# Wide moving operands in the first FFN's partial sums and in the mixer's projections

## The chip, the cores and the metric

The kernel runs on one core of a Trainium2 chip. The metric is device time in microseconds (us) of one execution; the shown time is the median of three runs. The engines are TensorE (PE: matmuls; its weight loads are PEld in the profile), VectorE (DVE), ScalarE (ACT), GpSimd (POOL) and SyncE (SP, which here only issues DMAs).

## The reference

One residual block on 256 tokens of width 2048, batch 1, all in float32. `mod` is a LayerNorm followed by a scale and a shift that are computed from a conditioning vector `c`.

```python
mod = (jax.nn.silu(c) @ w_ada[l] + b_ada[l]).reshape(B, N_SUBLAYERS, 3, D_MODEL)
y = _swiglu(modulate(x, 0), ffn1_w13[l], ffn1_w2[l])        # D_FF = 5632
x = _layer_norm(ALPHA * x + FFN_WEIGHT * gate[:, 0, None, :] * y, ln_g[l, 0], ln_b[l, 0])
u = modulate(x, 1)
proj = u @ w_in[l] + b_in[l]       # q, k, v, o, gates, x_rg, g_rg
h_m = _mlstm(...)                  # 4 heads of 256
h_r = _rg_lru(_causal_depthwise_conv(x_rg, ...), ...) * jax.nn.gelu(g_rg)
y = jnp.concatenate([h_m, h_r], axis=-1) @ w_out[l]
x = _layer_norm(ALPHA * x + gate[:, 1, None, :] * y, ln_g[l, 1], ln_b[l, 1])
y = _swiglu(modulate(x, 2), ffn2_w13[l], ffn2_w2[l])
x = _layer_norm(ALPHA * x + FFN_WEIGHT * gate[:, 2, None, :] * y, ln_g[l, 2], ln_b[l, 2])
```

with `_swiglu(u, w13, w2) = (silu(u @ w13_g) * (u @ w13_v)) @ w2`.

## The kernel before, in words

**Two-part products.** Every weight tile (128 x 2048 floats, 1 MB) is loaded by SP into one of four raw buffers, cast by ACT into a high part (line 95) and completed by DVE with a low part, the difference (line 97); there are three buffers of each part. The activations u are kept in two parts as well, `uh` and `ul` (lines 158 and 159), with the contraction on partitions: 16 blocks (KT) of 128 rows by 256 tokens. A product is three matmuls: high x high, high x low, low x high.

**Two forms of matmul.** In `stat_w` (lines 259 to 268) a block of 128 x 128 weights is stationary and the 256 tokens move: 128x256 out, features on partitions. In `mov_t` (lines 270 to 280) 128 tokens are stationary and 512 columns of weights move: 128x512 out, tokens on partitions. The profile tells them apart by line (266 to 268, 277 to 279).

**The conditioning.** Rows of w_ada are 144 tiles of 1 MB ("ada"), each multiplied with silu(c) and summed along the row by one DVE instruction (line 173). They go through the same SP queue and the same four raw buffers as the weights. `tick` (line 181) is called at each weight load and slips in ada tiles at a set rate per load: `RAMP_RATE` for each stage of the ramp, `FFN1_RATE` in the rest of the first FFN, `MIX_RATE` and `FFN2_RATE` later. `ada_until` issues at once all that a following step needs. Scale and shift of one block of u need two ada tiles.

**The ramp** (lines 571 to 647). The first FFN can't have all of u at its start, since u needs 32 ada tiles. So the first 24 of its 44 row blocks (each 128 columns of gate and of value) are worked off in five stages over the contraction: `STAGES` = 2, 2, 4, 4, 4 of the 16 blocks of u. A stage goes through 12 quads (2 row blocks, gate and value, in two PSUM banks) with `stat_w`. At the end of a quad its two sums are copied by ACT (first stage, line 642) or added by DVE (line 644) into a buffer in SBUF: the space of yacc, gate and x serves for that. Quads 6 and 7 instead keep four of the eight PSUM banks over the whole ramp. Shortly before a stage ends, `modulate` (lines 232 to 247) makes the next stage's blocks of u: transposes on PE, scale and shift and the high part on ACT, the low part on DVE. `EARLY` names the quads whose first block runs before the second block of u is there. In the last stage `swiglu` (line 554) turns each finished sum into the two-part h: Silu on ACT, product on DVE, high part on ACT, low part on DVE. Quads 8 to 11 get theirs in `g1(2)` (line 653), and x is loaded again there through ACT's queue, because its space was in use.

**The rest of the first FFN** takes blocks of 512 columns with `mov_w` (`rows_block`). Its h comes out with tokens on partitions, so `turn_one` (line 538) transposes it: four transposes on PE behind a given matmul, a copy on ACT (551), a subtraction on DVE (552). `g2` multiplies with w2 and adds into yacc.

**The mixer.** `proj` (line 778) makes 32 blocks of 128 features (x_rg, g_rg, k, q) with `stat_w`, two blocks in one PSUM bank, and ACT copies each out with its bias (784). Between them stand the gates, the convolution, the recurrence and the heads, mostly DVE work.

**The order.** Each engine runs its instructions in one order. It is laid by a planner, which simulates the program with its own costs before it is compiled; instructions given through `A`, `V`, `G`, `T` (line 125) keep the program's order, and `issue_after` puts one behind another.

Of the kernel before, what the change touches and what calls it, by code (L numbers as in the profile page):

```python
# [11 lines left out]
F32 = mybir.dt.float32  # L12
# [4 lines left out]
P = 128  # L17
# [34 lines left out]
def block_kernel(ctx: ExitStack, tc: tile.TileContext, a: dict, out: bass.AP):  # L52
# [105 lines left out]
    uh = big.tile([P, KT, S], F32R, name="uh")  # L158
    ul = big.tile([P, KT, S], F32R, name="ul")
# [109 lines left out]

    def mov_t(ps, hl, acth, actl, k0, t, first, last):  # L270
# [20 lines left out]
    def rows(k):  # L291

        return lambda: [u[:, k:k + 8, :].rearrange("p a b -> p (a b)") for u in (uh, ul)]
# [211 lines left out]
    def ffn(s, w13, w2, start, following=None):  # L505
# [4 lines left out]
        to_turn = []  # L510
        evac = []
# [6 lines left out]
        def rows_block(b, pg=None):  # L518
# [13 lines left out]
            for t in range(NT):  # L532
                sg = sm.tile([P, 512], F32, tag="u", bufs=2, name=f"sg{s}{b}{t}")
                nc.scalar.activation(sg, pg[t], AF.Silu)
                nc.vector.tensor_mul(sg, sg, pv[t])
                to_turn.append((b, t, sg))
# [16 lines left out]

        def swiglu(j, g, v, nm):

            sg = sm.tile([P, 512], F32, tag="u", bufs=2, name="sg" + nm)
            nc.scalar.activation(sg, g, AF.Silu)
            nc.vector.tensor_mul(sg, sg, v)
            hth, htl = hts[j // GRP]
            i = j % GRP  # L560
            dh = hth[:, i:i + 2, :].rearrange("p a b -> p (a b)")
            nc.scalar.copy(dh, sg)
            nc.vector.tensor_sub(htl[:, i:i + 2, :].rearrange("p a b -> p (a b)"), sg, dh.bitcast(F32))


        quads = RAMP // 2
        room = [r[:, 1024 * i:1024 * (i + 1)] for r in (*yacc, gate) for i in range(2)] + [None] * 2
        room += [x[:, i // 2, 1024 * (i % 2):1024 * (i % 2 + 1)] for i in range(quads - 8)]
        part = [r is not None and (r[:, 0:512], r[:, 512:1024]) for r in room]

        def ramp(ns):
# [4 lines left out]
            for st, k in enumerate(STAGES):  # L576
# [5 lines left out]
                per = 4 // k  # L582
# [3 lines left out]
                def tile_of(q):  # L586
                    nonlocal n_w
                    if q // per not in hls:
                        hls[q // per] = load_w(a["w13_r"][n_w], f"ra{n_w}")
                        n_w += 1  # L590
                    return hls[q // per]

                def banks(q):
                    if q in (6, 7):
                        if first:
                            kept[q] = (bank(f"kg{q}"), bank(f"kv{q}"))
                        return kept[q]
                    return bank(f"rg{st}_{q}"), bank(f"rv{st}_{q}")

                def products(q, pss, j0, nj, one):  # L600


                    hl = tile_of(q)
                    for i in range(4):
                        a0, a1 = j0 == 0, j0 + nj == k
                        if q in kept:
                            a0, a1 = a0 and first, a1 and last
                        if one or q in kept:
                            a0, a1 = a0 and i % 2 == 0, a1 and i % 2 == 1
                        stat_w(pss[i // 2][:, (i % 2) * S:(i % 2 + 1) * S], hl,  # L610
                               (((q % per) * 4 + i) * k + j0) * P, k0 + j0, nj, a0, a1)

                if first:
# [6 lines left out]
                    for q in EARLY:  # L620
                        held[q] = banks(q)
                        products(q, held[q], 0, 1, True)
                        if q == EARLY[0]:
                            rest()
                    ada_until(0, 1, 1)
                    modulate(0, ns, 1, 1)
                for q in range(quads):
                    if q == quads - per and not last:
                        k1 = k0 + k
                        ada_until(0, 1, k1 + STAGES[st + 1] - 1)  # L630
                        modulate(0, ns, k1, STAGES[st + 1])
                    if q in held:
                        pss = held[q]
                        products(q, pss, 1, k - 1, True)
                    else:
                        tile_of(q)
                        pss = banks(q)
                        products(q, pss, 0, k, False)
                    if q not in kept:
                        for ps, p in zip(pss, part[q]):  # L640
                            if first:
                                nc.scalar.copy(p, ps)
                            else:
                                nc.vector.tensor_add(p, p, ps)
                    if last and q < 8:
                        swiglu(2 * q, *(kept.get(q) or part[q]), f"r{q}")
                k0 += k

        def g1(gi):
            grp = groups[gi]  # L650
            if start and gi == 2:
                new_h(gi)
                for q in range(8, quads):
                    swiglu(2 * q, *part[q], f"r{q}")
# [495 lines left out]
```

## Time and profile before

| | |
|---|---|
| median of three runs | 1962.3 us (1961.88, 1962.3, 1964.59) |
| profiled execution, its own time | 1961.0 us |
| its span, first to last instruction | 1959.2 us |
| granted TensorE clock, mean over the span | 0.989 |
| busy share: PE, DVE, ACT, POOL | 97%, 72%, 43%, 2% |
| HBM read over the span | 509.22 MB, 261 GB/s |
| first and last product of the ramp | 20.7 and 317.4 us |
| first and last product of `proj` | 849.7 and 1093.7 us |

In the timeline each line gives start, length, engine, source line, operation and the names of what is written and read; in square brackets stands the idle time of the engine just before, and what ended it. Matmul lengths overlap: the next one begins before the one before has ended.

### The profile page before, as it was taken

How to read it: one execution, taken by the hardware profiler on the slowest of the kernel's cores; microseconds unless marked ns; L12 is line 12 of the kernel's file. 1: busy time of each engine (PE TensorE's matmuls, PEld its weight loads, DVE VectorE, ACT ScalarE, POOL GpSimd, SP SyncE). 2: the span in 40 equal slices, each digit the busy share in tenths (PEclk: the TensorE clock that was granted, in tenths of full speed). 3: DMA queues.
4: the chain of work that ended last, by engine and by line, in shares of the span. 5: the costliest groups of instructions: out<-in, count | busy, mean ns of one | idle time of the engine just before them, and what ended most of it. 6: DMA issues, size and time to landing. Idle time of an engine off the chain costs nothing.

```text
span 1959.2 us, 24619 instructions
## 1 busy us (share of the span) xinstructions
PE 1905.4 (97%) x10296; PEld 1649.1 (84%) x10296; DVE 1414.5 (72%) x1327; ACT 845.4 (43%) x812; POOL 34.9 (2%) x59
## 2 busy tenths in 40 slices
PE   6899999999999999899999998999999999999997
PEld 6899999888888888699999885788888888888885
DVE  7998898877867988688976886565555644544656
ACT  5343344533334335745643346444444333343340
POOL 0000000000000000000000120000000000000000
PEclk8999999999999999999999999999999999999998
DMA  9998888999788896388687673566666655554562
GB/s 367 346 349 315 308 316 327 336 334 346 297 313 313 309 348 251 129 324 287 232 298 288 230 271 130 209 248 244 246 242 250 231 193 191 193 194 172 194 216 85
DMA packets 72688, 512.91 MB, mean 262 GB/s; under 512 B 8449, under 2 KB 8577, under 8 KB 10881
## 3 DMA queue, kind: packets, MB, share of 16 engines
q1 hardware_dynamic: 70848, 507.54, 71.0%
q10 hardware_dynamic: 1728, 3.80, 0.6%
q8 instruction: 80, 1.31, 0.2%
q14 instruction: 32, 0.25, 0.0%
HBM read 509.22 MB, written 2.10 MB: 261 GB/s over the span
## 4 chain that ended last, share of the span: by engine, by line
PE 87%; DVE 6%; ACT 3%; DMA 2%; issue 1%; POOL 0%; DVEq 0%; SPq 0%; ACTq 0%
PE fv L278 6%; PE fv L279 6%; PE py L279 6%; PE py L277 6%; PE py L278 6%; PE fv L277 6%; PE fg L279 6%; PE fg L277 6%; PE fg L278 6%; PE pj L266 3%; PE pj L267 3%; PE pj L268 3%; PE tl L277 2%; PE tl L278 2%; PE tl L279 2%; PE rg L268 2%
## 5 line engine op out<-in xcount | busy, mean ns | idle before, releaser
L173 DVE CUSTOM_DVE_ANT_0 ada<-ada,scb,badac 128x2048 f32<-128x2048 f32 x144 | 337.8, 2348 | 92.3 <-DMA ada<-in_w_ada 89.8
L97 DVE TENSOR_TENSOR lw<-rw,hw 128x2048 fp32r<-128x2048 f32 x80 | 183.0, 2290 | 117.8 <-ACT hw L95 117.8
L95 ACT CAST hw<-rw 128x2048 fp32r<-128x2048 f32 x80 | 153.1, 1913 | 237.7 <-PE py L279 115.2
L97 DVE TENSOR_TENSOR lfv<-rfv,hfv 128x2048 fp32r<-128x2048 f32 x64 | 146.5, 2291 | 132.0 <-ACT hfv L95 132.0
L95 ACT CAST hfg<-rfg 128x2048 fp32r<-128x2048 f32 (+1 forms) x64 | 117.1, 1833 | 202.6 <-PE fv L279 79.2
L95 ACT CAST hfv<-rfv 128x2048 fp32r<-128x2048 f32 x64 | 122.4, 1912 | 185.2 <-PE fg L279 136.8
L278 PE MATMUL fv<-lfv,uh 128*128 128x512 f32 x512 | 200.5, 392 | 1.5 <-DVE lfv L97 1.5
L277 PE MATMUL fv<-hfv,uh 128*128 128x512 f32 x512 | 199.7, 391 | 2.3 <-ACT hfv L95 2.3
L97 DVE TENSOR_TENSOR lfg<-rfg,hfg 128x2048 fp32r<-128x2048 f32 x60 | 137.2, 2290 | 89.2 <-ACT hfg L95 89.2
L279 PE MATMUL fv<-hfv,ul 128*128 128x512 f32 x512 | 200.2, 391 | 0.0
L279 PE MATMUL py<-hw,htl 128*128 128x512 f32 x512 | 199.3, 389 | 0.0
L278 PE MATMUL py<-lw,hth 128*128 128x512 f32 x512 | 199.2, 389 | 0.0
L277 PE MATMUL py<-hw,hth 128*128 128x512 f32 x512 | 198.8, 392 | 0.0
L277 PE MATMUL fg<-hfg,uh 128*128 128x512 f32 x496 | 194.5, 393 | 0.0
L279 PE MATMUL fg<-hfg,ul 128*128 128x512 f32 x496 | 193.2, 389 | 0.0
L278 PE MATMUL fg<-lfg,uh 128*128 128x512 f32 x496 | 193.1, 389 | 0.0
L95 ACT CAST hra<-rra 128x2048 fp32r<-128x2048 f32 (+1 forms) x51 | 91.9, 1807 | 146.4 <-PE rv L267 72.7
L266 PE MATMUL pj<-uh,hs 128*128 128x256 f32 x512 | 145.3, 284 | 0.0
L267 PE MATMUL pj<-ul,hs 128*128 128x256 f32 x512 | 144.9, 283 | 0.0
L268 PE MATMUL pj<-uh,ls 128*128 128x256 f32 x512 | 144.9, 283 | 0.0
L97 DVE TENSOR_TENSOR lra<-rra,hra 128x2048 fp32r<-128x2048 f32 (+1 forms) x51 | 110.1, 2163 | 13.0 <-ACT hra L95 12.9
L278 PEld LDWEIGHTS fv<-lfv,uh 128*128 128x128 f32 x512 | 96.8, 189 | 22.8 <-DVE lfv L97 2.7
(380 smaller groups left out, 4120.7 us busy)
## 6 DMA issues: line engine op xcount, KB each, us to landing
ada<-in_w_ada SPq DMA_DIRECT2D x144, 1024.0 KB, 5.4
rw<-in_w SPq DMA_DIRECT2D x80, 1024.0 KB, 4.9
rfg<-in_w SPq DMA_DIRECT2D x64, 1024.0 KB, 4.9
rfv<-in_w SPq DMA_DIRECT2D x64, 1024.0 KB, 5.0
rra<-in_w_r SPq DMA_DIRECT2D x48, 1024.0 KB, 6.6
rs<-in_w_s SPq DMA_DIRECT2D x32, 1024.0 KB, 5.0
rwo<-in_w_out SPq DMA_DIRECT2D x16, 1024.0 KB, 4.9
ro<-in_w_vo SPq DMA_DIRECT2D x8, 1024.0 KB, 6.2
```

The lines of the kernel that those rows point to most:

```text
L95: act.copy(cut(hi, w), like(raw[:, w], hi))
L97: low.tensor_sub(cut(lo, w), like(raw[:, w], lo), cut(hi, w).bitcast(F32))
L173: nc.vector.tensor_tensor_reduce(raw, raw, scb, 1.0, badac[:, s, j, kt:kt + 1], ALU.mult, ALU.add, adac[:, s, j, kt:kt + 1])
L266: nc.tensor.matmul(ps, hi[:, w], uh[:, k0 + j, :], start=st, stop=False)
L267: nc.tensor.matmul(ps, hi[:, w], ul[:, k0 + j, :], start=False, stop=False)
L268: nc.tensor.matmul(ps, lo[:, w], uh[:, k0 + j, :], start=False, stop=sp)
L277: nc.tensor.matmul(o, acth[:, k0 + j, tk], cut(hi, w), start=first and j == 0, stop=False)
L278: nc.tensor.matmul(o, acth[:, k0 + j, tk], cut(lo, w), start=False, stop=False)
L279: end = nc.tensor.matmul(o, actl[:, k0 + j, tk], cut(hi, w), start=False, stop=last and j == 3)
```

## The change

*The ramp.* Its stages become 2, 3, 3, 4, 4 blocks of u. Tokens are stationary now: the 24 row blocks are six blocks b of 512 columns, each with p = 0 (gate) and p = 1 (value), and each (b, p) takes two banks, one for each half of the tokens. A 1 MB tile holds four pieces of 128 x 512 weights, so with three blocks in a stage a product straddles tiles. Block 3 keeps its four banks. The finished sums have tokens on partitions: `swiglu` (Silu and product) now only makes what `turn_one` turns, one for each (b, p) in the last stage. The last two blocks are made through `to_make`, two at once in `g1(2)` and two behind later turns. Loading x again and scaling it move from `g1(2)` to `g1(3)`. The rates of the ada tiles change.

*The mixer.* Both parts of u lie side by side in one tensor `u2`. In `stat_u` the high weights meet both parts in one matmul of 512 columns; the low weights meet the high part in one of 256. The two halves of the bank are added on the way out: ACT copies the first with the bias, DVE adds the second. `gates`, `rg_gates` and the rest are called behind the same blocks as before. The gate projection (`pif`) stays on `stat_w`.

```diff
-STAGES = (2, 2, 4, 4, 4)
+STAGES = (2, 3, 3, 4, 4)
-EARLY = (0, 1, 2)
-RAMP_RATE = (0.67, 1.34, 0.67, 0.67, 0.9)
-FFN1_RATE = 0.68
+KEPT = 3
+EARLY = ((0, 0), (0, 1), (1, 0))
+RAMP_RATE = (1.0, 0.67, 0.89, 0.67, 0.75)
+FFN1_RATE = 0.71
...
-    uh = big.tile([P, KT, S], F32R, name="uh")
-    ul = big.tile([P, KT, S], F32R, name="ul")
+    u2 = big.tile([P, KT, 2, S], F32R, name="u2")
+    uh, ul = u2[:, :, 0, :], u2[:, :, 1, :]
...
+    def stat_u(ps, hl):
+        hi, lo = hl
+        for k in range(KT):
+            w = slice(k * P, (k + 1) * P)
+            nc.tensor.matmul(ps, hi[:, w], u2[:, k].rearrange("p w b -> p (w b)"), start=k == 0, stop=False)
+            nc.tensor.matmul(ps[:, 0:S], lo[:, w], uh[:, k, :], start=False, stop=k == KT - 1)
...
+        def swiglu(b, t, g, v):
+            sg = sm.tile([P, 512], F32, tag="u", bufs=2, name=f"sg{s}{b}{t}")
+            nc.scalar.activation(sg, g, AF.Silu)
+            nc.vector.tensor_mul(sg, sg, v)
+            to_turn.append((b, t, sg))
...
+            if to_make:
+                swiglu(*to_make.pop(0))
...
+                def products(b, p, pss, j0, j1):
+                    for t in range(NT):
+                        tk = slice(t * P, (t + 1) * P)
+                        for j in range(j0, j1):
+                            i = (2 * b + p) * k + j
+                            hi, lo = tile_of(i // 4)
+                            w = slice(i % 4 * 512, (i % 4 + 1) * 512)
+                            go = j == 0 and (first or b != KEPT)
+                            end = j == k - 1 and (last or b != KEPT)
+                            nc.tensor.matmul(pss[t], uh[:, k0 + j, tk], hi[:, w], start=go, stop=False)
+                            nc.tensor.matmul(pss[t], uh[:, k0 + j, tk], lo[:, w], start=False, stop=False)
+                            mm = nc.tensor.matmul(pss[t], ul[:, k0 + j, tk], hi[:, w], start=False, stop=end)
+                    return mm
...
+                for b in range(RAMP // 4):
+                    for p in range(2):
+                        if b == RAMP // 4 - 1 and p == (k > 2) and not last:
+                            k1 = k0 + k
+                            ada_until(0, 1, k1 + STAGES[st + 1] - 1)
+                            modulate(0, ns, k1, STAGES[st + 1])
...
+                        if b != KEPT:
+                            for t in range(NT):
+                                if first:
+                                    nc.scalar.copy(part[b, p][t], pss[t])
+                                else:
+                                    nc.vector.tensor_add(part[b, p][t], part[b, p][t], pss[t])
+                        turn_one(end)
+                    if last and b < 4:
+                        g, v = (kept if b == KEPT else {p: part[b, p] for p in range(2)}).values()
+                        for t in range(NT):
+                            swiglu(b, t, g[t], v[t])
...
+                to_make.extend((b, t, part[b, 0][t], part[b, 1][t]) for b in (4, 5) for t in range(NT))
+                for t in range(NT):
+                    swiglu(*to_make.pop(0))
+                return
+            if start and gi == 3:
                 for t in range(NT):
                     nc.scalar.dma_start(x[:, t, :], a["x"][t * P:(t + 1) * P, :])
                 scale_x()
...
         def proj(i0, n, dst, after=None):
-            for i in range(0, n, 2):
+            for i in range(n):
                 ps = bank(f"pj{i0 + i}")
-                for q in range(2):
-                    stat_w(ps[:, q * S:(q + 1) * S], load_w(a["w_s"][i0 + i + q], f"s{i0 + i + q}"))
-                for q in range(2):
-                    nc.scalar.activation(dst[:, i + q, -S:], ps[:, q * S:(q + 1) * S], AF.Identity,
-                                         bias=bq[:, i0 + i + q:i0 + i + q + 1])
+                stat_u(ps, load_w(a["w_s"][i0 + i], f"s{i0 + i}"))
+                nc.scalar.activation(dst[:, i, -S:], ps[:, 0:S], AF.Identity, bias=bq[:, i0 + i:i0 + i + 1])
+                nc.vector.tensor_add(dst[:, i, -S:], dst[:, i, -S:], ps[:, S:])
```

The host lays the ramp's weights out anew to match; the number of 1 MB tiles stays 48.

More of the change, by code (lines that the diff above doesn't have):

```diff
@@ L552, in turn_one @@
             nc.vector.tensor_sub(htl[:, i:i + 4, tk], ps, hth[:, i:i + 4, tk].bitcast(F32))
[L554 to L569, printed above, removed]
+            if to_make:
+                swiglu(*to_make.pop(0))
+        room = [r[:, 512 * i:512 * (i + 1)] for r in (*yacc, gate, x[:, 0, :], x[:, 1, :]) for i in range(4)]
+        part = {}
+        for b in range(RAMP // 4):
+            if b != KEPT:
+                for p in range(2):
+                    part[b, p] = [room.pop(0) for _ in range(NT)]
         def ramp(ns):
@@ L600, in products, with tile_of @@
[L600 to L611, printed above, removed]
+                def tile_of(i):
+                    if i not in hls:
+                        hls[i] = load_w(a["w13_r"][n_w + i], f"ra{n_w + i}")
+                    return hls[i]
@@ L619, in ramp @@
                     modulate(0, ns, 0, 1)
[L620 to L623, printed above, removed]
+                    for n, (b, p) in enumerate(EARLY):
+                        held[b, p] = banks(b, p)
+                        products(b, p, held[b, p], 0, 1)
+                        if n == 0:
                             rest()
```

74 lines of the change are left out of this document (26 added, 48 removed).

## The prediction

> **What bounds the kernel now.** I read the page first: the share of each engine, and the chain of work that ended last.
>
> ```profile
> span 1959.2 us, 24619 instructions
> ...
> PE 1905.4 (97%) x10296; PEld 1649.1 (84%) x10296; DVE 1414.5 (72%) x1327; ACT 845.4 (43%) x812; POOL 34.9 (2%) x59
> ...
> PE 87%; DVE 6%; ACT 3%; DMA 2%; issue 1%; POOL 0%; DVEq 0%; SPq 0%; ACTq 0%
> ...
> rra<-in_w_r SPq DMA_DIRECT2D x48, 1024.0 KB, 6.6
> rs<-in_w_s SPq DMA_DIRECT2D x32, 1024.0 KB, 5.0
> ```
>
> TensorE is the limit over the span. The change touches two stretches: the ramp (48 weight tiles rra) and the mixer's projections (32 tiles rs). So I read the ramp next, as busy time of each engine in stretches that end where its stages end. The columns are length, busy time of PE, weight load, DVE, ACT and POOL with instruction counts, granted clock, DMA share, GB/s.
>
> ```profile
> 20.70:61.00 40.30, 38.95 (x295) 38.22 (x296) 33.75 (x27) 23.89 (x30) 0.00 (x0) 0.93 0.98 371
> 61.00:106.00 45.00, 39.39 (x285) 37.13 (x284) 43.87 (x42) 16.45 (x14) 0.00 (x0) 0.92 0.96 346
> 106.00:178.00 72.00, 71.96 (x601) 71.78 (x600) 65.42 (x58) 26.01 (x20) 0.00 (x0) 1.00 0.91 333
> 178.00:248.00 70.00, 69.46 (x580) 69.25 (x579) 60.09 (x51) 25.73 (x18) 0.00 (x0) 1.00 0.84 309
> 248.00:317.40 69.40, 69.40 (x580) 69.40 (x580) 67.47 (x67) 31.30 (x28) 0.00 (x0) 1.00 0.86 314
> 317.40:760.00 442.60, 442.60 (x1992) 367.21 (x1991) 354.07 (x293) 187.31 (x143) 0.00 (x0) 1.00 0.88 326
> ```
>
> The reader is to see two regimes. Up to 106 us the DMA share is 0.96 to 0.98: the weights and the ada tiles arrive too slowly. From 106 us on PE has no gap. DVE is never far behind: 43.87 of 45.00 in the second stage, 67.47 of 69.40 in the last.
>
> The stage ends come from the timeline and from the list of one tile's instructions. Line 243 makes u for the next stage while one tile's products are still to run, so a stage ends some 5 to 7 us after it.
>
> ```profile
> 51.78 1.90 ACT L95 CAST hra<-rra 128x2048 fp32r<-128x2048 f32 x1
> 54.66 1.02 ACT L243 ACTIVATE u<-tu,adac 128x256 f32<-128x256 f32 x2
> ...
> 61.16 0.59 ACT L642 COPY x<-rv 128x512 f32<-128x512 f32 x1 [0.61 <-PE rv L268]
> ...
> 98.81 1.92 ACT L243 ACTIVATE u<-tu,adac 128x256 f32<-128x256 f32 x4
> ...
> 173.17 1.92 ACT L243 ACTIVATE u<-tu,adac 128x256 f32<-128x256 f32 x4
> ...
> 243.15 1.93 ACT L243 ACTIVATE u<-tu,adac 128x256 f32<-128x256 f32 x4
> ...
> L266 PE MATMUL rv<-uh,hra x320: 278/283/416, 21.1 to 317.4; 128*128 128x256 f32 x160
> ```
>
> **The change, part by part.** First the price of a product. Durations of pipelined matmuls overlap, so I take start to start: 16 steps of the 256-wide form, then 24 steps of the 512-wide one.
>
> ```profile
> 900.06 0.28 PE L266 MATMUL pj<-uh,hs 128*128 128x256 f32 x1
> ...
> 901.98 0.28 PE L267 MATMUL pj<-ul,hs 128*128 128x256 f32 x1
> ...
> 1249.77 0.39 PE L277 MATMUL fv<-hfv,uh 128*128 128x512 f32 x1
> ...
> 1255.21 0.39 PE L277 MATMUL fv<-hfv,uh 128*128 128x512 f32 x1
> ```
>
> That is 1.92/16 = 0.1200 us and 5.44/24 = 0.2267 us. Two narrow products cost 0.2400, a wide one 0.2267: 0.0133 us saved for each pair. The mean durations (0.283 and 0.391) would have promised 0.175; the overlap makes them useless here. A ramp tile goes from 48 narrow products, 5.76 us, to 24 wide ones, 5.44 us. The wide form with tokens stationary already runs in fg and fv, so its price is no guess. The mixer's mixed pair (wide, then narrow) does not occur before; I take 0.2267 + 0.1200. Its bounds are the narrow price for all (no saving) and all at the wide rate for each column (0.340 for the pair).
>
> The Trainium skill, page "TensorE: Matmul & The Clock Gate", section "Back-to-back issue gap", speaks against the change: it gives an isolated product N/2.4 + 2.5 ns, so two narrow ones would lose only 2.5 ns to one wide one. Over the 1152 + 512 pairs here that is an estimate of 4.2 us by the page, against 22.1 us by the rows; the rows' fixed cost is 13 ns, not 2.5, and they decide.
>
> DVE has to keep up, and its prices are start to start as well.
>
> ```profile
> 89.70 2.35 DVE L173 CUSTOM_DVE_ANT_0 ada<-ada,scb,badac 128x2048 f32<-128x2048 f32 x1
> ...
> 91.97 2.35 DVE L173 CUSTOM_DVE_ANT_0 ada<-ada,scb,badac 128x2048 f32<-128x2048 f32 x1
> ...
> 107.03 0.68 DVE L644 TENSOR_TENSOR x<-x,rg 128x512 f32<-128x512 f32 x1
> 107.63 0.68 DVE L644 TENSOR_TENSOR x<-x,rv 128x512 f32<-128x512 f32 x1
> ...
> 302.53 2.29 DVE L97 TENSOR_TENSOR lra<-rra,hra 128x2048 fp32r<-128x2048 f32 x1
> 304.74 0.68 DVE L644 TENSOR_TENSOR x<-x,rg 128x512 f32<-128x512 f32 x1
> ```
>
> An ada tile costs 2.27 us, a partial sum's add (or any op of 512 columns) 0.60, a tile's low part 2.21. A tile on DMA costs 1.049 MB at some 0.36 MB/us, 2.9 us. A stage lasts as long as the busiest of the three. I tried this on the old stages. Stage 1 has 6 tiles and, at rate 1.34, 8 ada tiles: PE 34.6, DMA 14 x 2.9 = 40.6, DVE 13.3 + 18.2 + 20 adds 12.0 + 0.6 = 44; it took 45. Stages 2 and 3 (12 tiles, 8 ada): PE 69.1 + 0.8 of transposes = 70, DVE 58, DMA 58; they took 72 and 70. Stage 4: PE 69.1, DVE 72, and it took 69.4, with some DVE work left for later. The rule holds within 2 to 3 us.
>
> The new stages by the same rule:
> - Stage 0 ends on weights that land late. With rate 1.0 there are 10 ada tiles ahead of its sixth weight tile instead of 8, or one more than the queue already sent early: 2.9 to 5.8 us later. I take +4: 65.4 instead of 61.4.
> - Stage 1 (9 tiles, 6 ada): PE 49.0 + 0.6, DVE 46.7, DMA 43.5: 49.6.
> - Stage 2 (9 tiles, 8 ada): PE 49.6, DVE 19.9 + 18.2 + 12.0 + 1.2 = 51.3, DMA 17 x 2.9 = 49.3: 51.3.
> - Stage 3 (12 tiles, 8 ada): PE 65.3 + 0.8, DVE and DMA 58: 66.1.
> - Stage 4 (12 tiles, 9 ada): the activations now come out with tokens on partitions and have to be turned; four transposes cost 0.35 us:
>
> ```profile
> 459.26 0.60 PE L549 MATMUL th<-ident,sg 128*128 128x128 f32 x4
> 459.61 0.47 PE L277 MATMUL fg<-hfg,uh 128*128 128x512 f32 x1
> ```
>
> Eight turns in the ramp are 2.8 us of PE: 65.3 + 2.8 = 68.1. DVE: 26.5 + 20.4 + 12.0 + 9.6 for SwiGLU = 68.5.
>
> The sum is 300.9. I add 3 us, because stages 1, 2 and 4 have two or three resources within 3 us of each other, which the old stages 2 to 4 mostly had not; the bounds are 0 and the 13 us that make the ramp end where it ends now. The ramp ends near 304 instead of 317.4: **13.4 us gained**. The copy and subtraction behind each turn replace a copy and a subtraction of the same size. Weight tiles that straddle two products in the stages of 3 are held a third of a product longer; three buffers cover it, and without that cover it would be the 2 us by which such a tile's release is late.
>
> The four remaining turns fall into FFN work where PE has no gap: 4 x 0.35 = **1.4 us lost**. The rate 0.71 moves some 3 ada tiles (7 us of DVE) into 317 to 760 us, where DVE has 88 us free: nothing. The reload of x by ACT's queue comes one group later; ACT is busy 187 of 442 us there and x is first used two groups on, so nothing; without that cover it would be 2.1 MB, 6 us.
>
> The mixer: 32 tiles x 16 pairs x 0.0133 = **6.8 us gained**. It adds 32 DVE additions out of PSUM. The stretches are the projections xr and gg, then v, then k and q.
>
> ```profile
> 842.00:952.00 110.00, 110.00 (x887) 108.67 (x886) 97.36 (x113) 65.59 (x80) 0.11 (x1) 1.00 0.78 283
> 952.00:992.00 40.00, 40.00 (x183) 33.30 (x183) 39.58 (x38) 20.33 (x21) 0.11 (x1) 1.00 0.74 260
> 992.00:1066.00 74.00, 74.00 (x598) 72.92 (x596) 49.01 (x31) 28.05 (x24) 0.00 (x0) 1.00 0.80 297
> ...
> 1118.85 0.40 DVE L976 TENSOR_TENSOR og<-og,pn 128x256 f32<-128x256 f32 x1
> ```
>
> Line 976 is the same operation at the same size: 0.40. For xr and gg that is 16 x 0.36 (between 0.33 and 0.40) = 5.8 us, where DVE has 110 + 40 - 97.4 - 39.6 = 13.1 us free and loses 3.4 to the shorter span: 3.9 us remain. Hidden, but barely; I take **1 us lost** for an add that waits at the head of DVE with a low part behind it, between 0 and the last rival. For k and q 25 us are free.
>
> Sum: 13.4 + 6.8 - 1.4 - 1 = 17.8 us. The profiled execution took 1961.0 (1.8 around its span); the runs shown have a median of 1962.3, 1.3 above it. So 1961.0 - 17.8 + 1.3 = 1944.5, and I say **1944**.
>
> **The rivals.**
> 1. *The ramp becomes PE's alone*: the new stage sizes remove the early waits. Then 20.7 + 48 x 5.44 + 6 of transposes + 2.8 + 3 of slow clock = 294, 23 gained; in all 23 + 6.8 - 1.4 = 28: 1934. For it: 0.92 of clock and 5.6 us of PE idle in the second stage. Against: DMA is full until 106 us, and the change asks it for more in stage 0.
> 2. *DVE becomes the bound in the ramp*. It is busy 270.6 of 296.7 us there, and its work hardly changes. If it waits as long as now (26 us), the ramp ends 3 us earlier at most; with the mixer's part 7 in all: 1955. For it: the last stage already at 97%. Against: half of that waiting was for PE, which now comes sooner.
> 3. *The wide product saves nothing in its new places* (paced at 0.2400). The stages become 65.4, 52.4, 52.4, 69.9, 71.9, with the 3 us 315; with the turns and no gain in the mixer about 0: 1962. Against: the fv row above, with tokens stationary too, keeps 0.2267. (The Trainium skill's rule quoted above would come close to this.)
> 4. *Slower: the new add blocks DVE in xr and gg.* The add needs ACT's copy of the same tile; where that stands behind a cast of 1.9 us the add waits up to 2.3 us, and DVE's low parts, conv and gates stand behind it. 16 x 2.3 = 37 against 3.9 free: 33 lost, 14 more than all gains: 1976. It costs from 0.24 us a wait, and turns the sign from 1.4 us. For it: DVE 99% busy in 952 to 992. Against: the planner may put other DVE work ahead of the add, and low parts are made two tiles ahead.
>
> **How the numbers follow.** Forecast (1938 to 1950) 0.48, rival 1 0.12, rival 2 0.22, rival 3 0.07, rival 4 0.11. The range 1932 to 1957 takes in the forecast and the first two and leaves out 0.18. No change means within 0.2%, 4 us, about what a measurement here can tell. Faster: 0.48 + 0.12 + 0.20 = 0.80; same 0.10; slower 0.10.
>
> **What the new profile would show.** The wide ramp products 0.227 us apart, and mixer tiles 5.55 us apart instead of 5.76. The last ramp product near 304, not 294 or 314. u of stage 1 made near 59, where it was 55. DVE above 95% from 61 us to the ramp's end. The mixer's stretch from first to last pj product shorter by 6 to 7 us, with no PE idle put down to DVE. The forecast is wrong if the early DMA stretch grows by more than 6 us, if PE shows idle behind low parts in the ramp, or if the waits of DVE for the copies of the projections (line 784 before) add up to over 20 us.

## The result and the profile after

| | before | changed |
|---|---|---|
| median of four runs | 1962.6 us | 1948.8 us (1947.0 to 1952.9) |
| ratio, with its 95% interval | | 0.9931 [0.9912, 0.9949] |
| profiled execution, its span | 1959.2 us | 1948.4 us |
| last product of the ramp begins | 317.7 | 307.2 |
| first product of `proj` begins | 849.7 | 841.2 |
| last product of `proj` begins | 1094.0 | 1083.0 |

The first measurement puts the gain at 0.5 to 0.9%. Two later ones gave 0.9932 [0.9914, 0.9949] and 0.9952 [0.9935, 0.997]. (The ramp's and `proj`'s last products, 317.4 and 1093.7 in the table of the kernel before, are those of the first of the three product lines; here the last of all three is taken.) In the profiled executions the span is 10.8 us shorter: the ramp brings 10.5, the rest of the first FFN takes 2.0 back, `proj` brings 2.5 and what follows takes 0.2. One of the ten runs of old_stages, further down, took 8557.75 us; its median there is that of the other nine.

The page of the changed kernel, with the chain of work that ended last:

```profile
span 1948.4 us, 21414 instructions
...
PE 1890.1 (97%) x8680; PEld 1562.7 (80%) x8680; DVE 1425.4 (73%) x1360; ACT 845.6 (43%) x813; POOL 37.0 (2%) x59
...
PE 84%; DVE 8%; ACT 3%; DMA 3%; issue 2%; POOL 0%; DVEq 0%; SPq 0%; ACTq 0%
```

PE is busy 15 us less and still sets the end, but the chain has 3 points less of PE and 2 more of DVE. Busy time in stretches that end where the new stages end (columns as before). The ends are rounded; the last product of a stage, counted off in the timeline (72 products for each block of u, 144 before), begins at 67.6, 117.4, 170.2, 238.2 and 307.2 us (before: 60.8, 107.5, 177.8, 248.5, 317.7).

```profile
20.20:68.00 47.80, 41.62 (x153) 32.40 (x154) 40.23 (x33) 27.47 (x37) 0.00 (x0) 0.84 0.98 381
68.00:118.00 50.00, 50.00 (x224) 41.27 (x223) 46.63 (x41) 20.02 (x16) 0.00 (x0) 1.00 0.90 336
118.00:170.00 52.00, 49.60 (x222) 40.61 (x221) 51.81 (x50) 20.17 (x15) 0.00 (x0) 1.00 0.93 347
170.00:238.00 68.00, 66.50 (x298) 54.95 (x297) 61.05 (x53) 25.84 (x18) 0.00 (x0) 1.00 0.86 326
238.00:307.40 69.40, 69.40 (x323) 57.50 (x322) 67.00 (x68) 32.14 (x30) 0.00 (x0) 1.00 0.81 299
68.00:307.40 239.40, 235.49 (x1062) 194.34 (x1061) 226.48 (x209) 98.17 (x78) 0.00 (x0) 1.00 0.87 325
```

The third stage is DVE's: 51.81 of 52.00. Over the four stages behind the first DVE is busy 226.5 of 239.4 us, and PE 235.5: neither has much room. The timeline of the ramp: casts and weight issues in stage 0, the matmul that waited there and two products behind it, the later makings of u (line 246 is what line 243 was) and the waits at them, and three casts of tiles in stage 3; then the last row of tile rv's list.

```profile
49.64 2.60 SPq L87 DMA_DIRECT2D rra<-in_w_r  x2
...
54.34 1.49 ACT L246 ACTIVATE u<-tu,adac 128x256 f32<-128x256 f32 x3
56.51 3.72 ACT L97 CAST hra<-rra 128x2048 fp32r<-128x2048 f32 x2
...
58.48 0.87 PE L617 MATMUL rg<-hra,u 128*128 128x512 f32 x2 [4.01 <-ACT hra L97]
...
62.25 0.63 PE L618 MATMUL rg<-lra,u 128*128 128x512 f32 x1
62.68 0.63 PE L619 MATMUL rg<-hra,u 128*128 128x512 f32 x1
...
114.01 1.47 ACT L246 ACTIVATE u<-tu,adac 128x256 f32<-128x256 f32 x3
...
164.79 1.01 ACT L246 ACTIVATE u<-tu,adac 128x256 f32<-128x256 f32 x2
...
165.86 0.66 PE L242 MATMUL tu<-ident,n 128*128 128x128 f32 x4 [1.79 <-ACT u L246]
...
181.55 1.92 ACT L97 CAST hra<-rra 128x2048 fp32r<-128x2048 f32 x1 [3.52 <-PE rv L619]
186.99 1.92 ACT L97 CAST hra<-rra 128x2048 fp32r<-128x2048 f32 x1 [3.52 <-PE rg L619]
192.43 1.92 ACT L97 CAST hra<-rra 128x2048 fp32r<-128x2048 f32 x1 [3.52 <-PE rv L619]
...
232.32 1.47 ACT L246 ACTIVATE u<-tu,adac 128x256 f32<-128x256 f32 x3
232.86 0.47 PE L617 MATMUL rv<-hra,u 128*128 128x512 f32 x1 [1.50 <-DVE x L654]
...
L619 PE MATMUL rv<-hra,u x160: 387/389/628, 24.2 to 307.2; 128*128 128x512 f32 x160
```

A tile takes 5.44 us (181.55, 186.99, 192.43): 24 products of 0.2267. That is the forecast's price to the last digit. The waits behind the start are few and short; the largest is in stage 0, 4.01 us for the cast of the sixth weight tile. The products behind it are 0.43 us apart (62.25, 62.68) at a granted clock of 0.50 (60 to 64 us), where the kernel before has 1.00, so the stretch behind the wait costs time as well.

The mixer: lists of the tiles pj and pv and of the new add, then timeline rows of two groups of pairs, of two PE waits and of what DVE did ahead of the first, and the window in which DVE has no gap.

```profile
L278 PE MATMUL pj<-u,hs x512: 387/395/578, 841.2 to 1082.7; 128*128 128x512 f32 x171
L279 PE MATMUL pj<-u,ls x512: 274/280/388, 841.4 to 1083.0; 128*128 128x256 f32 x171
...
L288 PE MATMUL pv<-hv,u x64: 389/389/476, 944.7 to 987.7; 128*128 128x512 f32 x64
...
L799 DVE TENSOR_TENSOR xr<-xr,pj x8: 401/402/418, 857.4 to 897.3; 128x256 f32<-128x256 f32 x8
...
859.93 0.40 PE L278 MATMUL pj<-u,hs 128*128 128x512 f32 x1
...
863.81 0.40 PE L278 MATMUL pj<-u,hs 128*128 128x512 f32 x1
...
865.34 2.35 DVE L176 CUSTOM_DVE_ANT_0 ada<-ada,scb,badac 128x2048 f32<-128x2048 f32 x1 [2.42 <-DMA ada<-in_w_ada]
...
868.28 2.27 DVE L99 TENSOR_TENSOR ls<-rs,hs 128x2048 fp32r<-128x2048 f32 x1
...
870.61 0.39 PE L279 MATMUL pj<-u,ls 128*128 128x256 f32 x1 [0.74 <-DVE ls L99]
...
915.64 0.67 PE L884 MATMUL pr<-xc,wax 128*128 128x256 f32 x2 [0.86 <-DVE gg L799]
...
1010.06 0.39 PE L278 MATMUL pj<-u,hs 128*128 128x512 f32 x1
...
1012.83 0.39 PE L278 MATMUL pj<-u,hs 128*128 128x512 f32 x1
...
880.00:910.00 30.00, 29.60 (x170) 25.53 (x169) 30.00 (x44) 14.88 (x10) 0.00 (x0) 1.00 0.80 281
```

Eleven pairs from 859.93 to 863.81 are 0.353 us apart, eight from 1010.06 to 1012.83 are 0.346 (0.3467 within the rounding of the stamps): both paces occur. From the first pj to the first pv, that is in xr and gg, 103.0 us became 103.5; from the first pv to the last pj, that is in v, k and q, 141.3 became 138.3. All that the mixer gains is gained behind gg. At 865.34 DVE has stood idle 2.42 us for an ada tile to land; the low part ls behind it is ready only when PE already waits for it (870.61).

### The profile page after: what moved, and what is told of

Its sections match the earlier page's. It is cut to its first block, busy times and chain, and to the rows that moved or that the text cites. A ratio compares the mean times of both kernels' runs of the same rounds, so it can differ in the third digit from the quotient of the medians.

```text
span 1948.4 us, 21414 instructions
## 1 busy us (share of the span) xinstructions
PE 1890.1 (97%) x8680; PEld 1562.7 (80%) x8680; DVE 1425.4 (73%) x1360; ACT 845.6 (43%) x813; POOL 37.0 (2%) x59
## 4 chain that ended last, share of the span: by engine, by line
PE 84%; DVE 8%; ACT 3%; DMA 3%; issue 2%; POOL 0%; DVEq 0%; SPq 0%; ACTq 0%
PE fv L289 6%; PE fv L290 6%; PE py L290 6%; PE py L288 6%; PE py L289 6%; PE fv L288 6%; PE fg L290 6%; PE fg L288 6%; PE fg L289 6%; PE pj L278 4%; PE pj L279 2%; PE rv L618 2%; PE rv L617 2%; PE rg L619 2%; PE rg L618 2%
## 5 line engine op out<-in xcount | busy, mean ns | idle before, releaser
L289 PE MATMUL fv<-lfv,u 128*128 128x512 f32 x512 | 200.2, 391 | 2.0 <-DVE lfv L99 2.0
L288 PE MATMUL fv<-hfv,u 128*128 128x512 f32 x512 | 199.1, 390 | 2.3 <-ACT hfv L97 2.3
L290 PE MATMUL fv<-hfv,u 128*128 128x512 f32 x512 | 199.8, 390 | 0.0
L288 PE MATMUL fg<-hfg,u 128*128 128x512 f32 x496 | 195.4, 394 | 0.0
L290 PE MATMUL fg<-hfg,u 128*128 128x512 f32 x496 | 193.7, 390 | 0.0
L289 PE MATMUL fg<-lfg,u 128*128 128x512 f32 x496 | 193.5, 390 | 0.0
L278 PE MATMUL pj<-u,hs 128*128 128x512 f32 x512 | 179.6, 396 | 0.0
L279 PE MATMUL pj<-u,ls 128*128 128x256 f32 x512 | 142.7, 279 | 1.1 <-DVE ls L99 1.1
L289 PEld LDWEIGHTS fv<-lfv,u 128*128 128x128 f32 x512 | 96.5, 188 | 22.9 <-DVE lfv L99 2.9
L288 PEld LDWEIGHTS fv<-hfv,u 128*128 128x128 f32 x512 | 96.4, 188 | 22.8 <-ACT hfv L97 2.7
```

The costliest lines, as they stand in the source:

```text
L278: nc.tensor.matmul(ps, hi[:, w], u2[:, k].rearrange("p w b -> p (w b)"), start=k == 0, stop=False)
L279: nc.tensor.matmul(ps[:, 0:S], lo[:, w], uh[:, k, :], start=False, stop=k == KT - 1)
L288: nc.tensor.matmul(o, acth[:, k0 + j, tk], cut(hi, w), start=first and j == 0, stop=False)
L289: nc.tensor.matmul(o, acth[:, k0 + j, tk], cut(lo, w), start=False, stop=False)
L290: end = nc.tensor.matmul(o, actl[:, k0 + j, tk], cut(hi, w), start=False, stop=last and j == 3)
```

## The experiments

All in one table. "Ramp" is the start of the last ramp product, "xr, gg" the time from the first pj to the first pv, both from the profiled execution, as is the span. Ratios are to the kernel before on the same chip.

| run | median us | ratio [95%] | ramp | first pj | xr, gg | last pj | span |
|---|---|---|---|---|---|---|---|
| changed, first | 1948.8 | 0.9931 [0.9912, 0.9949] | 307.2 | 841.2 | 103.5 | 1083.0 | 1948.4 |
| ramp_only | 1952.4 | 0.9951 [0.9937, 0.9966] | 308.5 | 845.3 | 103.1 | 1089.7 | 1955.7 |
| mixer_only | 1957.5 | 0.9973 [0.9963, 0.9982] | 317.6 | 849.7 | 101.0 | 1088.9 | 1956.2 |
| old_stages | 1960.8 | 0.9987 [0.9975, 0.9999] | 313.1 | 854.4 | 101.0 | 1093.6 | 1959.3 |
| tile_first | 1948.4 | 0.9935 [0.992, 0.995] | 306.5 | 842.0 | 101.2 | 1081.4 | 1946.3 |
| again (changed) | 1950.6 | 0.9932 [0.9914, 0.9949] | 305.9 | 839.8 | 102.6 | 1080.7 | 1947.4 |
| no_ada_xrgg | 1955.4 | 0.9958 [0.9944, 0.9973] | 305.9 | 839.8 | 101.2 | 1079.9 | 1953.3 |
| late_ada | 1959.2 | 0.998 [0.9968, 0.9993] | 300.3 | 838.7 | 101.0 | 1077.9 | 1955.8 |
| spread_ada | 1946.5 | 0.9923 [0.9907, 0.994] | 301.2 | 838.1 | 101.2 | 1077.5 | 1942.0 |
| half_ada | 1945.1 | 0.9913 [0.9894, 0.9932] | 303.1 | 842.0 | 101.0 | 1081.3 | 1947.4 |
| narrow_xrgg | 1952.1 | 0.9949 [0.9934, 0.9964] | 306.9 | 840.8 | 103.1 | 1083.4 | 1950.6 |
| after_5 (changed) | 1951.5 | 0.9952 [0.9935, 0.997] | 307.8 | 841.7 | 102.7 | 1082.6 | 1947.6 |
| half_5 (half_ada) | 1944.4 | 0.991 [0.9897, 0.9923] | 304.5 | 838.5 | 101.0 | 1077.7 | 1942.3 |

### Each part alone

*ramp_only* is the changed kernel with the old projections; *mixer_only* is the kernel before with u2, `stat_u` and the new projections.

```diff
 ramp_only, against the changed kernel
-            for i in range(n):
+            for i in range(0, n, 2):
 ...
-                stat_u(ps, load_w(a["w_s"][i0 + i], f"s{i0 + i}"))
 ...
+                for q in range(2):
+                    stat_w(ps[:, q * S:(q + 1) * S], load_w(a["w_s"][i0 + i + q], f"s{i0 + i + q}"))
 ...
 mixer_only, against the kernel before: the same two places the other way round
```

> The ramp as changed, the projections of the mixer as before (three narrow products, copied out by ACT alone). Theory A (the gain is the ramp's, and the mixer gives next to nothing because DVE has no room for its adds): the last ramp product near 307, the stretch from the first to the last projection product back at 244 us, time 8 to 10 us under the kernel before, 1952 to 1955. Rival B (the mixer's part gives its 6 us, and the ramp's end is worth less than its 10 us): time 3 to 6 us under the kernel before, 1957 to 1960.

> The mixer's projections as changed, the ramp as before. Theory A: the stretch from the first to the last projection product is 241 to 242 us (244.3 before), nearly all of it from k and q, and 1.5 to 3 us are gained: 1960 to 1961. Rival B: 6 us gained, 1957. Rival C (the adds hold DVE up more than the products save): slower than before by 1 us or more.

Lists of the ramp and of pj, of the first kernel and then of the second:

```profile
L617 PE MATMUL rv<-hra,u x160: 389/389/628, 22.7 to 308.0; 128*128 128x512 f32 x160
...
L271 PE MATMUL pj<-u,ls x512: 278/283/283, 845.6 to 1089.7; 128*128 128x256 f32 x171
```

```profile
L276 PE MATMUL pj<-u,ls x512: 274/280/284, 849.9 to 1088.9; 128*128 128x256 f32 x171
...
L285 PE MATMUL pv<-hv,u x64: 389/389/475, 950.7 to 993.6; 128*128 128x512 f32 x64
```

By their ratios the ramp alone gained 0.49%, 9.6 us, and the mixer alone 0.27%, 5.3 us. In mixer_only `proj` went from 244.3 to 239.2 us: 5.1. Together they would give 15; the changed kernel gained 13.8, and its `proj` only 2.5 in the first profiled execution and 3.4 in the two others (240.9 us). In mixer_only xr and gg take 101.0 us and no wait of PE stands between the first and the last pj. So the wide form does pay in xr and gg, 2.1 us (103.1 with the old form, in ramp_only); beside the new ramp it is lost to waits. The first kernel's time is that of theory A, but A's reason, that the mixer gives next to nothing, fails: the second kernel's 5.3 us are nearest to rival B.

### The wide form without the new stages

```diff
 old_stages, against the changed kernel
-STAGES = (2, 3, 3, 4, 4)
+STAGES = (2, 2, 4, 4, 4)
-RAMP_RATE = (1.0, 0.67, 0.89, 0.67, 0.75)
-FFN1_RATE = 0.71
+RAMP_RATE = (0.67, 1.34, 0.67, 0.67, 0.9)
+FFN1_RATE = 0.68
```

> The changed kernel with the stages 2, 2, 4, 4, 4 and the rates of the ada tiles of the kernel before. Theory A (the ramp's gain is that of the wide form, tile by tile; the stage sizes only move waits from the second stage into the first): stage 0 ends near 61 instead of 68, the second stage is bound by DVE and DMA again (45 us for two blocks of u), and the ramp ends within 4 us of 307: 1945 to 1953. Rival B (the stage sizes bring the gain): the ramp ends at 313 or later, 1955 or more.

Two windows of it, the third stage and the last, and the largest of its waits of PE for DVE between 70 and 1200 us, in the ramp and in the FFN (released by; us in total, times, longest):

```profile
104.00:174.00 70.00, 69.04 (x310) 56.95 (x309) 66.32 (x58) 27.79 (x20) 0.00 (x0) 1.00 0.93 347
241.00:313.00 72.00, 70.82 (x327) 58.35 (x327) 71.02 (x72) 32.25 (x30) 0.00 (x0) 1.00 0.85 314
...
PE rv L617 <- DVE x L654: 2.7, 1, 2.7
...
PE fg L289 <- DVE lfg L99: 2.1, 3, 1.4
...
PE py L289 <- DVE lw L99: 1.5, 1, 1.5
```

With tokens stationary but the old stages and rates little is gained: 0.13%, 2.6 us. And this kernel has the new projections, which by themselves gave 5.3 (mixer_only). On the same chip its median is 3.3 us above that of mixer_only (the intervals, [0.9975, 0.9999] and [0.9963, 0.9982], just overlap): the ramp's wide form without the new stages saves no time, and may cost some. The ramp does end 4.6 us earlier, not 10.5. Its last stage has 11 ada tiles (12 x 0.9) and all of SwiGLU, and DVE is busy 71.02 of 72.00 there; PE waits 2.7 us for an add of DVE. What DVE has not done by then is late in the FFN: PE waits for the low parts lfg and lw, 3.6 us, and 541.3 us pass from the ramp's end to the first pj where the kernel before needs 532.0 and the changed one 534.0. The waits shown are not all of these 9.3 us; the rest is open. The gain of the ramp's part thus needs the new stage sizes and rates. No run has these with the old form, so what they would bring alone is not shown. My theory, that the matmul form carries it, fell.

### Is DVE the ramp's bound?

In *tile_first* the sixth weight tile of stage 0 goes ahead of the remaining ada tiles; in *late_ada* the last stage is also relieved of six ada tiles.

```diff
 tile_first, against the changed kernel
-RAMP_RATE = (1.0, 0.67, 0.89, 0.67, 0.75)
+RAMP_RATE = (0.67, 0.67, 0.89, 0.67, 0.75)
                             k1 = k0 + k
+                            if first:
+                                tile_of(5)
                             ada_until(0, 1, k1 + STAGES[st + 1] - 1)
 late_ada, against tile_first
-RAMP_RATE = (0.67, 0.67, 0.89, 0.67, 0.75)
+RAMP_RATE = (0.67, 0.67, 0.89, 0.67, 0.25)
```

> The changed kernel, with stage 0 at rate 0.67 and its sixth weight tile issued ahead of the last ada tiles that stage 1 needs. Theory A (stage 0 ends at 68 because the sixth tile stands in SP's queue behind ten ada tiles: issued at 49.6, cast at 56.5): the sixth cast comes near 51, PE's wait of 4.0 us before it and the slow clock behind it go, stage 0 ends 4 to 6 us earlier, and 3 to 5 us of that are left at the ramp's end: 1944 to 1946. Rival B (DMA has to bring the same tiles before stage 1 can end anyway): stage 0 ends earlier, stage 1 as late as now, time within 2 us of 1949.

> The kernel with the sixth tile first, and the rate of the last ramp stage 0.25 instead of 0.75: six ada tiles, 14 us of DVE work, leave the last stage. Theory A (behind stage 1 DVE sets the ramp's pace and swallows the 5 us that the first stage gains): from the making of the last u to the ramp's end 74 us instead of 76.7, PE's waits for adds and for the low parts of h gone, ramp end 303 to 304; the time 1945 to 1947. Rival B (PE's own work sets the last stage): ramp end 305 to 307, time as without it.

tile_first: the window from 64 us to the ramp's end.

```profile
64.00:306.50 242.50, 236.21 (x1049) 192.50 (x1048) 231.21 (x212) 97.61 (x77) 0.00 (x0) 0.99 0.88 331
```

late_ada: the last stage, and two rows of PE's waits.

```profile
230.00:300.00 70.00, 70.00 (x326) 58.01 (x325) 60.34 (x60) 32.12 (x31) 0.00 (x0) 1.00 0.67 246
...
PE tl L288 <- ACT hwo L97: 6.4, 1, 6.4
...
PE tl L289 <- DVE lwo L99: 1.1, 1, 1.1
```

In tile_first stage 0 ended 9.8 us earlier (its last product at 57.8 instead of 67.6), more than expected. Then the u of stage 2 came 6 us earlier (107.97 instead of 114.01), that of stage 3 four, that of stage 4 under three; the ramp's end moved by 0.7, and the time not at all, as rival B has it. The start's gain is eaten on the way. DVE is busy 231.2 of 242.5 us; but in stage 1, which takes 5 us back, ACT's casts also wait 22.6 us for weight tiles to land (4.0 in the changed kernel), which is rival B's reason, and the two are not told apart there. The last stage takes another 4 us back (72.8 us instead of 69.0), with no cast waiting for DMA.

late_ada shows what that last part hangs on. With six ada tiles (13.6 us of DVE) out of the last stage that stage has no wait of PE, DVE is busy 60.34 of 70.00, and the ramp ends 6.2 us earlier. Of these, 3.7 us are the last stage's (69.1 instead of 72.8); 2.5 came before it, where both kernels have the same rates: at 161.88 tile_first waits 2.23 us for u and has a clock of 0.50 from 163 to 166 us, late_ada waits 0.90 us and keeps 1.00. But the tiles fell due together where the mixer needs the scale and shift for its end: seven ada tiles are issued in a row ahead of the next weights wo, PE waits 6.4 + 1.1 us for these, and the median is 8 to 10 us above the changed kernel's. Work that is moved must be moved to a place of its own.

### What costs xr and gg their gain?

```diff
 no_ada_xrgg, against the changed kernel
+        credit[1] = 0.0                 (ahead of the projection xr)
+        credit[1] = 0.85                (behind gg)
 narrow_xrgg, against the changed kernel: the old proj for the first 16 blocks, the new for k and q
-        proj(1, 8, xr, {1: gates})
+        proj_n(1, 8, xr, {0: gates})
 ...
-        proj(9, 8, gg, {3: rg_gates, 5: lambda: (gate_cols(), recurrence())})
+        proj_n(9, 8, gg, {2: rg_gates, 4: lambda: (gate_cols(), recurrence())})
```

> The changed kernel unaltered, a second time. The stretch of the projections xr and gg (first projection product to first product of v) took 103.0 us before, 103.5 in the changed kernel, 101.0 with the mixer's part alone. Theory A (the 2.5 us belong to the order of the instructions, which is fixed): 103 to 104 again. Rival B (they belong to the one execution: late DMAs): 101 to 102. The time: 1947 to 1951, the ramp's end 306 to 309.

> The changed kernel with no ada tiles during the projections xr and gg, and rate 0.85 instead of 0.55 behind them. Theory A (DVE has no room for the adds in xr and gg): with some 20 us of DVE work taken out of that stretch it falls to 99 to 100 us, the 3.4 us that 16 tiles should save, and 1 to 4 us are left of it in the time: 1945 to 1948. Rival B (each add waits for ACT's copy, whatever else DVE has to do): 101 us or more, time not under that of the changed kernel.

> The changed kernel with the old form (256 columns throughout, two blocks in a bank, ACT copies both out, no add) for the first 16 blocks of proj, x_rg and g_rg; k and q as changed. Theory A (the wide form gains nothing in these two, since DVE is full there and the adds make PE wait): the same time as the changed kernel, within 1.5 us, 1948 to 1951, first pj to first pv 102.5 to 104 us and the PE waits behind gg and the low parts there gone or moved. Theory B (the wide form's 16 x 16 x 0.0133 = 3.4 us are gained and something else costs the stretch its time): 2 to 4 us slower, 1951 to 1954, first pj to first pv 105 to 107 us.

no_ada_xrgg, a row of PE's waits; behind it the lists of pj and pv of narrow_xrgg; then DVE's waits for ada tiles from the first pj to the first pv, in the changed kernel and in old_stages:

```profile
PE pn L974 <- DVE misc L966: 6.6, 1, 6.6
```

```profile
L278 PE MATMUL pj<-u,hs x256: 389/398/478, 982.6 to 1083.2; 128*128 128x512 f32 x128
...
L288 PE MATMUL pv<-hv,u x64: 389/389/475, 943.9 to 987.1; 128*128 128x512 f32 x64
```

```profile
DVE ada L176 <- DMA ada<-in_w_ada: 7.3, 4, 2.5
```

```profile
DVE ada L176 <- DMA ada<-in_w_ada: 4.5, 4, 1.6
```

Run again, the changed kernel takes 102.6 us there, and 102.7 as after_5, with two of the three waits of PE at the same places: it is not one execution's chance. With four ada tiles in the stretch instead of ten, all late in gg, PE has no wait there and it takes 101.2 us: 1.4 less than in "again", 2.3 less than in the first profile, the level of mixer_only. So it is the ada tiles, though they cost less than the 3.4 us expected. The ada tiles behind gg then made the heads wait 6.6 us, and the kernel lost 5. With the old form there (narrow_xrgg) the stretch is 103.1 and has no wait either, against 102.6, 102.7 and 103.5 in the three profiles of the changed kernel: between -0.4 and 0.5 us, the wide form is worth nothing in xr and gg of the changed kernel, and 2.1 us (101.0) where no wait comes. The medians (ratios 0.9949 against 0.9931, 0.9932 and 0.9952) don't tell the two kernels apart.

What is it about the ada tiles? Neither their number nor the order on DVE: old_stages runs the same 121 instructions of DVE in the same order there, with as many ada tiles, and takes 101.0 without a wait. What differs is when the tiles land. DVE stands idle for them 7.3, 6.8 and 6.9 us in the three profiles of the changed kernel, and 4.5 us or less in every other kernel here, none of which has a wait of PE in the stretch. In the order laid for DVE the low parts and the adds stand behind the ada tiles, and are late with them (865.34 to 870.61 above). That these waits cause the loss is read from such rows; no run moves the landing alone. Why the tiles land later in the changed kernel stays open.

### A better spread

```diff
 spread_ada, against late_ada
-FFN1_RATE = 0.71
+FFN1_RATE = 0.78
 half_ada, against late_ada
-RAMP_RATE = (0.67, 0.67, 0.89, 0.67, 0.25)
-FFN1_RATE = 0.71
+RAMP_RATE = (0.67, 0.67, 0.89, 0.67, 0.5)
+FFN1_RATE = 0.75
```

> The kernel of late_ada (sixth weight tile of stage 0 ahead of the ada tiles, rate 0.25 in the ramp's last stage), but the rate in the rest of the first FFN raised from 0.71 to 0.78, over 84 weight tiles some 6 ada tiles: those that the last stage gave up are worked off there, not at the end of the mixer. Theory A: they are hidden in the rest of the first FFN, where DVE was busy 364 of 452.6 us and gets 6 x 2.27 = 13.6 us more. Then the ramp ends near 300.3 as in late_ada, first pj 534 us behind it (as in the changed kernel), 834 to 836, last pj near 1075, no wait of 6 us of PE in the heads or at the mixer's end, span near 1942: 1943 to 1945 us. Theory B: DVE's time is free there only on the average; the low parts of weights stand behind the ada tiles and PE waits for them, 1 us at a time, until the gain is gone: first pj at 840 to 842 again, 1948 to 1951 us.

> As spread_ada, with half of it: rate 0.5 in the ramp's last stage (3 ada tiles more in it than with 0.25, 6.8 us of DVE) and 0.75 in the rest of the first FFN. Theory A (DVE paces the ramp's last stage, and the ada tiles are hidden behind it): ramp end about 303, the last pj near 1077 to 1079, 1946 us. Theory B (the rest of the first FFN gives back what it gets): the same time as the changed kernel, 1949 to 1951 us, whatever the ramp's end.

> The changed kernel, unaltered, beside half_ada on one chip, five rounds each. Theory A (moving ada tiles out of the ramp's last stage is worth what the ramp's end shows, 303.1 instead of 305.9 to 307.2): 1949 to 1951 us, 3 to 5 us above half_ada. Theory B (the difference of the medians so far, 1945.1 and 1946.5 against 1948.8 and 1950.6, is scatter between executions, which reaches 9 us for half_ada): within 1.5 us of half_ada.

> half_ada, unaltered, beside the changed kernel on one chip, five rounds each. Theory A: 1944 to 1947 us, 3 to 5 us below the changed kernel. Theory B: within 1.5 us of it.

spread_ada and half_5: the window in which the moved tiles run, for each.

```profile
310.00:760.00 450.00, 450.00 (x2031) 373.28 (x2030) 374.19 (x320) 188.92 (x151) 0.00 (x0) 1.00 0.89 338
```

```profile
310.00:760.00 450.00, 450.00 (x2030) 373.33 (x2029) 367.59 (x312) 190.80 (x152) 0.00 (x0) 1.00 0.89 337
```

PE has no gap in either window, with 374.19 and 367.59 us of DVE where the changed kernel has 361.57 (same window): in these two executions the tiles are hidden. (From the ramp's end to the first pj spread_ada still takes 536.9 us, 2.9 more than the changed kernel and more than its theory A said; 2.51 of them are one wait for u at 800.2 us, which tile_first and late_ada have as well.) half_5 against after_5, on one chip, is 1944.4 against 1951.5 us, and its interval [0.9897, 0.9923] lies below [0.9935, 0.997]. Of the 5.3 us between the two spans, 3.3 come from the ramp and 1.7 from xr and gg, whose waits are gone. Both kernels also have tile_first's order in stage 0; the new spread was not run without it. The profiled execution of half_ada, the same kernel as half_5, had its first pj at 842.0, 3.5 us later than half_5, with waits for low parts in the FFN that half_5 has not: the order holds with little to spare. Both kernels with a better spread have medians below the changed one's. For half_ada the runs on one chip show that it is faster; spread_ada was not run beside the changed kernel, and the intervals of the two overlap.

## Why the prediction was right, and where it was not

The forecast was 1944 us, a gain of 17.8 in the span; it was 1948.8 and 10.8 (11.8 and 11.6 in the two later profiles). The direction, the two sources and their order of size were right. No error made up for another: in the first profile the ramp is short by 2.9 us, the mixer by 3.3, the FFN by 0.6 and what follows by 0.2. Point by point:

**The price of a ramp tile**: 5.44 us, measured 5.44. Taking it start to start, and not from the durations, was right. Of the two prices for the pair of narrow products, the fixed cost of 2.5 ns that the Trainium skill ("TensorE: Matmul & The Clock Gate", "Back-to-back issue gap") gives for an isolated product and 13 ns by the rows, the ramp's 5.44 us against 5.76 bears the rows out.

**The ramp, 13.4 us**: measured 10.5 by the starts of the last products (317.7 to 307.2), then 11.8 and 9.9. By stages, forecast and measured: 65.4 and 68.0 (end of stage 0), 49.6 and 50.0, 51.3 and 52.0, 66.1 and 68.0, 68.5 and 69.4. The 3 us for coupling were about right (0.4 + 0.7 + 1.9 + 0.9 = 3.9). **The step furthest off is stage 0's "+4"**: the stage ended 6.6 us later than the old one. Eleven ada tiles were issued ahead of the sixth weight tile, nine before: the prediction's ten and eight are one too low each, their difference is right. The cast came 4.7 us later (56.51, was 51.78); the rest is PE behind it at a mean clock of 0.84 in that stretch (0.93 before). In the two later profiles the stage's last product begins at 66.1 and 65.0 us instead of 67.6, which is 5.3 and 4.2 later than before: there the "+4" is nearly right, and the ramp still falls short by 1.6 and 3.5 us. And tile_first shows that this term doesn't stand alone: with it mended the ramp's end moves by 0.7. A sum over stages, each by its busiest engine, hides that DVE has 226.5 of 239.4 us to do in them together, and late work in one stage is paid in the next.

**Which part of the ramp's change pays**: the prediction made a tile 0.32 us cheaper, 15.4 us for 48 tiles, and did not ask what this brings without the new stages. old_stages shows it: 4.6 at the ramp's end and, less what the projections give, nothing in the time. The rule of the busiest engine had the right tool (72 us of DVE in the old last stage) and I did not apply it to that half step.

**The turns, 1.4 us**: from the ramp's last product to the first pj 532.0 us became 534.0, 533.9 and 533.9. Right within 0.6; PE's waits in that stretch are the same (8.0 and 8.1 us).

**The mixer, 6.8 less 1**: 5.1 in mixer_only, 2.5 to 3.4 in the changed kernel. Two terms were mis-sized. The mixed pair was taken at 0.3467; it is that in about half of the tiles and 0.353 in the others: 512/2 x 0.0067 = 1.7 us, as much as 5.1 is short of 6.8. And "1 us lost" for waits in xr and gg is 1.7 to 2.6, and for another reason than the prediction gave. There, as in rival 4, the new add was to wait for ACT's copy and hold up DVE. In the profile no add of line 799 waits for a copy. DVE waits for ada tiles to land, and what stands behind them is late: PE waits for a low part (870.61) and for the add (915.64). This costs less than a tenth of what rival 4 priced; between 880 and 910 us DVE is busy throughout, but it is so for 30 us, not for 110.

**The rivals.** 1 (PE alone, 294) didn't occur; late_ada's 300.3 is the nearest to it. 2 (DVE becomes the bound) holds for the last stage, shown by tile_first and late_ada, but of its price, 10 us less of gain in the ramp, only 1.6 to 3.5 were missing, stage 0's share included. 3 (no gain from the wide product) is refuted by the rows. 4 is described above.

**What was to be seen**: products 0.227 us apart, yes; the ramp's end near 304, 307.2; u of stage 1 near 59, it was at 54.34, as before (54.66); DVE above 95%, 94.6% from 68 us on; mixer tiles 5.55 us apart, in the half that runs at 0.3467; `proj` shorter by 6 to 7 us with no wait for DVE, no on both. Two of the three signs of being wrong came, though the time stayed in the range: stage 0 grew by 6.6 us in the first profile, over the 6 that were allowed, and PE waits 0.6 us for a low part of the ramp at 60.81. The third, DVE waiting for the projections' copies, did not come.

## What to carry to other kernels

When PE and a second engine are both near full, price a change of the matmul's form with the whole stretch's load of the second engine, not stage by stage: here the faster products of the ramp saved no time until the stages and the side work were laid out for them. An engine's free time is no cover for work that waits for its own data at the engine's head: an ada tile that lands late holds up the low parts behind it. Side work that only has to be done at some time (the ada tiles here) belongs where the second engine has room, and wherever it is moved, look for the step that needs it next: the same six tiles cost 8 to 10 us where they fell due together (late_ada) and were free where DVE had room (spread_ada). Test each half of a double change alone: of the 5.1 us that the projections gave alone, half to two thirds were left beside the new ramp.

## What the runs showed of the hardware

A pair of a 512-wide and a 256-wide product with one weight load each runs at one of two paces, 0.3467 or 0.353 us. In each of three kernels followed pair by pair (mixer_only, half_5 and the changed one) the pace stays for tens of pairs and changes only where another matmul, a wait or two products of the same width in a row come between, as at 870.61 in the changed kernel. The shapes of the operands do not differ, and why there are two paces stays open. Executions of one kernel also differ by several us at the same landmarks: the ramp of the changed kernel ended at 305.9, 307.2 and 307.8, and its runs on one chip spread from 1947.6 to 1959.8 us as after_5, half_ada's from 1940.4 to 1949.2 on one chip and, as half_5, from 1943.7 to 1945.5 on another.
